# A flow backbone with three attention groups: transposes of each block of keys issued ahead of its predecessor's products, in groups B and C

## The chip, the cores and the metric

The kernel runs on one core of a Trainium2 chip. The metric is device time in microseconds (us) for one execution; less is better. Before the change the median of three runs is 1200.18 us (1199.35 to 1202.86).

## The reference

Two trunk layers work on 512 latent tokens (a grid of 8 rows by 64 columns) and 256 context tokens, each 1024 wide. A layer normalises and modulates both streams, projects them to queries, keys, values and gates, runs three groups of attention heads side by side, multiplies by a SiLU gate, projects back and adds. Context reads context alone; latents read their own keys and all context keys in one softmax. The second layer needs no context output.

```python
def layer(x, cx, ...):
    px, pc = split_cols(hx @ w_in), split_cols(hc @ w_in)
    ya, yca = global_gqa(...)          # A: 8 heads, 2 of keys; all 512 + 256 keys
    yb, ycb = neighbourhood_attn(...)  # B: 8 heads; 8 x 16 window with bias, + 256 keys
    yc_, ycc = window_gqa(...)         # C: 8 heads, 2 of keys; +-128 tokens, sink, + 256 keys
    ux = jnp.concatenate([ya, yb, yc_], -1) * jax.nn.silu(px[9])
    x = x + gate * (ux @ w_out)
```

All is in float32.

## The kernel before

**Precision.** A float32 operand that goes through TensorE is split in two of a faster type, a rounded part (names ending in h, or index x = 0) and the rest (l, or x = 1). So one float32 product is two or three matmuls.

**Stages.** `PLAN` (line 33) lists the stages of a layer. In each stage the attention of one pair of heads runs (B pairs 0 to 3, then A and C in turn: A0, C0, A1, C1, A2, C2, A3, C3) and beside it the projections that a later stage needs: beside B those of further B pairs and the first A pair, beside A those of a C pair, beside C those of an A pair. `weave` (line 1407) takes from the two generators in proportion to the microseconds that each of their steps yields. Behind the last stage the output projection starts (`head`, line 527).

**A unit.** A pair of heads is cut in units (`units`, line 1288): for each head one unit of 512 latent queries in B (`NearUnit`) and C (`BandUnit`), two units of 256 in A (`GlobalUnit`), and in the first layer one unit for the context queries (`CtxUnit`). A unit has two generators. `scores` makes the scores in PSUM (tile `Sbig`), their row minimum or maximum and the exponentials in SBUF (tile `P`, 128 queries each, five buffers). `values` turns them round and multiplies by the values. `attend` (line 1375) zips the values of one unit with the scores of the next.

**Values.** Keys come in six blocks of 128; blocks 4 and 5 are the context. For each block, the parts of `P` that have keys in it are transposed on TensorE into a PSUM bank (`turn`, line 1053; tile `T`, two banks, `psT`, line 96). `pt_copy` (line 1039) moves the bank to SBUF in two halves: ScalarE (ACT) copies the rounded half, `pth`, and VectorE (DVE) takes the difference, `ptl`, which needs the first. Three buffers hold each half. `pv` (line 1058) then multiplies the block's values by both halves into the accumulator `Obig`, one PSUM bank for all units. A block of group B has four query tiles (context) or two; one of C has four (context), two or three. `o_out` (line 1069) folds the two halves of the accumulator when the sixth block is done. The helper functions `mul` and `turn` record every product and every transpose, so in the profile all products stand at L1049 and all transposes of this kind at L1054; they are told apart by tiles.

The T banks are shared. The query transposes of an A pair's projection (`a_pair`, line 883, transposes at L899, copied out by ACT at L902 into tile `qt`) take one too, and so do `finish` (line 1315) and, once a layer, the keys of A and the values of C.

**Order.** The program is written with one issue order, but each engine's queue is laid out before the run by a planner that simulates a timeline (line 1666): the issue order is its priority, and where an instruction would not be ready in the simulation, a later one can go first. Some orders are fixed by hand with `after` (line 99): projections may not run further ahead of the attention than `lead` allows (lines 296 and 1407). On the chip every queue keeps the order that was laid out.

**Ahead.** The helper `ahead` (line 1098) takes steps of turns, sums and a time. It issues the turns of a step, yields, issues the sums of the step before, and yields. Only group A uses it before the change. In B and C a block's transposes and copies are issued, then a yield, then the same block's products, then a yield.

Of the kernel before, what the change touches and what calls it, by code (L numbers as in the profile page):

```python
# [771 lines left out]
def mixers(tc, nc, l, last, p1, ps, const, env):  # L772
# [19 lines left out]
    turns = {}  # L792

    def copy(out, src, kind):

        n = turns[kind] = turns.get(kind, -1) + 1
        if CFG[kind][n % len(CFG[kind])] == "A":
            nc.scalar.activation(out, src, AF.Copy)  # L798
        else:
            nc.vector.tensor_copy(out, src)  # L800
# [238 lines left out]
    def pt_copy(T, n):  # L1039

        hi = p1.tile([128, 512], F32R, name="pth", bufs=CFG["pt"])
        lo = p1.tile([128, 512], F32R, name="ptl", bufs=CFG["pt"])
        copy(hi[:, 0:n], T[:, 0:n], "cp")
        i = nc.vector.tensor_sub(lo[:, 0:n], T[:, 0:n], hi[:, 0:n].bitcast(F32))  # L1044
        pace["dve"] = i.ins.name
        return hi, lo

    def mul(*args, **kw):
        m = nc.tensor.matmul(*args, **kw)  # L1049
        pace["pe"] = m.ins.name  # L1050
        return m

    def turn(*args, **kw):
        m = nc.tensor.transpose(*args, **kw)  # L1054
        pace["pe"] = m.ins.name
        return m

    def pv(O, v, pt, o, c0, n, first, final):

        for x in range(2):  # L1060
            a = mul(O if c0 is None else O[:, c0:c0 + n], v, pt[x][:, o:o + n], start=first and x == 0,
                                 stop=final and x == 1, skip_group_check=True)

            if first and x == 0 and "last" in opv:
                after(a, opv["last"])
            if final and x == 1:
                opv["last"] = a.ins.name

    def o_out(O, OT, h, c0, n):
        tmp = p1.tile([64, 512], F32, name="otmp", bufs=1)  # L1070
        nc.scalar.activation(tmp[:, 0:n], O[64:128, 0:n], AF.Copy)
        nc.vector.tensor_add(OT[64 * h:64 * h + 64, c0:c0 + n], O[0:64, 0:n], tmp[:, 0:n])
# [25 lines left out]
    def ahead(steps):  # L1098


        late = None
        for turns, sums, t in steps:
            pt = turns()
            yield t
            if late:
                late[0](late[1])
                yield late[2]
            late = sums, pt, t
        late[0](late[1])
        yield late[2]  # L1110

    class CtxUnit(Unit):
# [18 lines left out]
        def values(self):  # L1131
            T = psT()
            for kb in range(2):
                for t in range(2):
                    turn(T[:, (2 * kb + t) * 128:(2 * kb + t + 1) * 128],
                                        self.P[:, t * 256 + kb * 128:t * 256 + (kb + 1) * 128], ident)
            pt = pt_copy(T, 512)
            yield 0.45
            O = half_O()
            for kb in range(2):  # L1140
                pv(O, self.v(4 + kb), pt, kb * 256, 0, 256, kb == 0, kb == 1)
            o_out(O, self.OT(), self.h, NT, NCX)
            yield 0.45
# [41 lines left out]
    class BandUnit(Unit):  # L1185
# [32 lines left out]

        def values(self):
            O = psO()  # L1220
            for n, kb in enumerate((4, 5, 0, 1, 2, 3)):
                qs = [i for i in range(4) if kb in self.pos[i]]
                T = psT()
                for j, i in enumerate(qs):
                    o = self.pos[i][kb]
                    turn(T[:, j * 128:(j + 1) * 128], self.P[i][:, o:o + 128], ident)
                k = len(qs) * 128
                pt = pt_copy(T, k)
                yield k / 1200
                pv(O, self.v(kb), pt, 0, qs[0] * 128, k, n == 0, n == 5)  # L1230
                yield k / 1200
            o_out(O, self.OT(), self.h, 0, NT)

    class NearUnit(Unit):
# [36 lines left out]

        def values(self):
            O = psO()
            for n, kb in enumerate((4, 5, 1, 2, 3, 0)):
                qs = [i for i in range(4) if kb in self.PLAN[i][4]]
                T = psT()
                for j, i in enumerate(qs):
                    o = self.PLAN[i][4][kb]
                    turn(T[:, j * 128:(j + 1) * 128], self.P[i][:, o:o + 128], ident)
                k = len(qs) * 128  # L1280
                pt = pt_copy(T, k)
                yield k / 1200
                out = O[:, qs[0] * 128:qs[0] * 128 + k] if kb else O.rearrange("p (t c) -> p t c", t=4)[:, 0:4:3]
                pv(out, self.v(kb), pt, 0, None, k, n == 0, n == 5)
                yield k / 1200
            o_out(O, self.OT(), self.h, 0, NT)

    def units(kind, i, Q, K, V, G, extra):
# [242 lines left out]
    for pair, items, n_ada in PLAN:  # L1531
# [3 lines left out]
        if pair is not None:  # L1535
            kind, i = pair
# [13 lines left out]
        t = sum(time[k] for k, i in items)  # L1550
# [120 lines left out]
```

## Time and profile before

| | us |
|---|---|
| median of three runs | 1200.18 |
| lowest, highest run | 1199.35, 1202.86 |
| span of the profiled execution | 1197.7 |
| TensorE busy | 1150.5 |
| TensorE weight loads | 1034.8 |
| VectorE busy | 769.4 |
| ScalarE busy | 696.9 |
| GpSimd busy | 408.1 |

The span is what the profile shows of its one execution, from the first to the last instruction; the time of a run has in addition what lies around it, and the lowest of the three is 1.65 us above the span, the median 2.5 us. In the rows of the profile, PE is TensorE (PEld its weight loads, which overlap with its matmuls), DVE is VectorE, ACT is ScalarE, POOL is GpSimd and SP issues DMAs. A row of the timeline has the start, the duration, the engine, the line, the operation, the tile written and the tiles read, the shape, how many instructions were merged, and in brackets the idle time of the engine before it and what ended that. Matmuls are pipelined: their ends are modelled, and one that follows another starts before the other's end. So a short stall of TensorE doesn't always appear as idle time.

### The profile page before, as it was taken

What the parts mean: (1) busy time and instruction counts of PE and PEld (TensorE: products, weight loads), DVE (VectorE), ACT (ScalarE), POOL (GpSimd) and SP (SyncE); (2) the same over time, 40 slices, a digit from 0 to 9 for tenths busy, and PEclk for the clock granted to TensorE, in tenths of its full rate; (3) what the DMA queues carried; (4) which work ended last, traced back from release to release, by engine and by line L of the source; (5) the groups of instructions that cost most, each with busy time, mean ns of one, the idle gap of its engine ahead of it and who ended that gap; (6) DMA issues with size and microseconds to landing.
All of it is one profiled execution on the core that took longest, in us unless ns stands there. A gap on an engine that the chain in (4) does not pass through costs nothing.

```text
span 1197.7 us, 21749 instructions
## 1 busy us (share of the span) xinstructions
PE 1150.5 (96%) x8016; PEld 1034.8 (86%) x8016; DVE 769.4 (64%) x1548; ACT 696.9 (58%) x1581; POOL 408.1 (34%) x496
## 2 busy tenths in 40 slices
PE   5999999999999999999999999999999999998997
PEld 3898999998898988988778999989988888887876
DVE  5767566764656665568578895567754556567563
ACT  5446555656666676588423544555666667677552
POOL 1341110234446354385000030202274563656001
PEclk9999999999999999999999999999999999999999
DMA  9552222313312112123086662323222111232152
GB/s 321 213 142 89 78 78 67 123 66 104 111 70 92 67 44 92 34 63 119 27 293 198 205 210 74 98 84 109 91 73 67 53 46 53 63 88 72 36 161 77
DMA packets 60826, 124.22 MB, mean 104 GB/s; under 512 B 7216, under 2 KB 13488, under 8 KB 60720
## 3 DMA queue, kind: packets, MB, share of 16 engines
q1 hardware_dynamic: 54768, 111.96, 29.6%
q10 hardware_dynamic: 5952, 10.88, 2.7%
q8 instruction: 63, 1.03, 0.3%
q14 instruction: 43, 0.35, 0.1%
HBM read 109.05 MB, written 11.14 MB: 100 GB/s over the span
## 4 chain that ended last, share of the span: by engine, by line
PE 81%; DVE 5%; ACT 5%; DMA 3%; issue 3%; POOL 1%; SPq 0%; ACTq 0%; DVEq 0%; POOLq 0%
PE pj L318 18%; PE pj L341 17%; PE Sbig L1049 9%; PE Obig L1049 9%; PE T L1054 9%; PE pj L519 5%; PE T L519 3%; PE Sbig L519 3%; PE T L341 2%; PE Sbig L430 2%; DVE ptl L1044 1%; DMA x<-xT_dram 1%; PE Sbig L341 1%; ACT pth L798 1%; PE pj L430 1%
## 5 line engine op out<-in xcount | busy, mean ns | idle before, releaser
L1044 DVE TENSOR_TENSOR ptl<-T,pth 128x512 fp32r<-128x512 f32 (+2 forms) x312 | 181.1, 591 | 128.6 <-ACT pth L798 126.7
L798 ACT ACTIVATE pth<-T 128x512 fp32r<-128x512 f32 (+2 forms) x312 | 158.9, 520 | 134.8 <-PE T L1054 128.1
L341 PE MATMUL pj<-wh,hL 128*128 128x256 f32 x896 | 180.6, 287 | 0.0
L318 PE MATMUL pj<-hL,wh 128*128 128x512 f32 x544 | 175.0, 401 | 0.9 <-ACT wh L247 0.5
L1054 PE MATMUL T<-ident,P 128*128 128x128 f32 x1024 | 165.7, 273 | 4.0 <-ACT qt L902 1.7
L247 ACT ACTIVATE wh<-ws 128x512 fp32r<-128x512 f32 x192 | 119.5, 629 | 78.6 <-PE pj L318 16.3
L1049 PE MATMUL Sbig<-kt,qt 128*128 128x256 f32 (+1 forms) x864 | 156.2, 308 | 4.6 <-ACT P L1160 2.5
L250 POOL TENSOR_TENSOR wl<-ws,wh 128x512 fp32r<-128x512 f32 x76 | 98.5, 1300 | 146.4 <-ACT wh L247 146.4
L341 PEld LDWEIGHTS pj<-wh,hL 128*128 128x128 f32 x896 | 144.2, 190 | 1.0 <-issue 0.2
L1049 PE MATMUL Obig<-pth,vt 128*128 128x256 f32 (+2 forms) x432 | 134.6, 321 | 4.6 <-ACT pth L798 2.0
L1054 PEld LDWEIGHTS T<-ident,P 128*128 128x128 f32 x1024 | 123.0, 140 | 17.6 <-DVE ptl L1044 2.2
L1049 PE MATMUL Obig<-ptl,vt 128*128 128x256 f32 (+2 forms) x432 | 131.4, 318 | 5.0 <-DVE ptl L1044 4.3
L1049 PEld LDWEIGHTS Sbig<-kt,qt 128*128 128x128 f32 x864 | 123.3, 189 | 13.4 <-DVE negm L1208 4.1
L341 PE MATMUL pj<-wl,hL 128*128 128x256 f32 x448 | 128.0, 286 | 0.0
L318 PEld LDWEIGHTS pj<-hL,wh 128*128 128x128 f32 x544 | 96.2, 189 | 16.7 <-ACT wh L247 0.9
L250 DVE TENSOR_TENSOR wl<-ws,wh 128x512 fp32r<-128x512 f32 x116 | 82.7, 720 | 40.4 <-ACT wh L247 31.6
L318 PE MATMUL pj<-hL,wl 128*128 128x512 f32 x272 | 107.1, 394 | 0.5 <-DVE wl L250 0.5
L1049 PEld LDWEIGHTS Obig<-pth,vt 128*128 128x128 f32 x432 | 81.6, 189 | 15.9 <-ACT pth L798 7.1
L1049 PEld LDWEIGHTS Obig<-ptl,vt 128*128 128x128 f32 x432 | 81.5, 189 | 14.7 <-DVE ptl L1044 11.3
L1445 POOL TENSOR_TENSOR bm<-wr,bm 128x192 f32<-128x192 f32 (+1 forms) x48 | 41.3, 888 | 139.6 <-DMA bm<-mskB_dram 132.4
L341 PEld LDWEIGHTS pj<-wl,hL 128*128 128x128 f32 x448 | 85.4, 191 | 0.3
L1158 DVE TENSOR_REDUCE negm<-Sbig 128x1 f32<-128x768 f32 x64 | 61.0, 953 | 29.7 <-PE Sbig L1049 15.7
(336 smaller groups left out, 2495.6 us busy)
## 6 DMA issues: line engine op xcount, KB each, us to landing
ws<-wf_dram SPq DMA_DIRECT2D x72, 256.0 KB, 3.1
ws<-wt_dram SPq DMA_DIRECT2D x72, 256.0 KB, 3.0
ada<-adaw_dram SPq DMA_DIRECT2D x32, 512.0 KB, 5.5
ws<-wo_dram SPq DMA_DIRECT2D x57, 256.0 KB, 2.8
bm<-mskB_dram SPq DMA_DIRECT2D x16, 576.0 KB, 3.7
dw<-adat_dram SPq DMA_DIRECT2D x8, 512.0 KB, 8.2
dots<-adat_dram SPq DMA_DIRECT2D x16, 256.0 KB, 4.5
u<-u ACTq DMA_DIRECT2D x9, 384.0 KB, 2.9
```

Of the source, the lines that this page charges most:

```text
L247: nc.scalar.activation(hi, src, AF.Copy)
L250: eng.tensor_sub(lo, src, hi.bitcast(F32))
L318: paced(nc.tensor.matmul(p[:, 0:n], a[:, r, :], cols(b[kt], c0, n), start=(i == 0), stop=(i == 23)), i)
L341: paced(nc.tensor.matmul(p[:, t * 256:(t + 1) * 256], tok(a[kt], t2 + t), b[:, r, :], start=(i == 0), stop=(i == 23)), i)
L430: mm = nc.tensor.matmul(out, a, b, start=begin, stop=(kt == KT - 1 and i == 2), skip_group_check=True)
L519: mm = nc.tensor.matmul(p[:, 0:n], a[:, r, :], ucols(ua[b][ft], c0, n), start=(ft == FT_ORDER[0] and i == 0), stop=(ft == FT_ORDER[-1] and ...
L798: nc.scalar.activation(out, src, AF.Copy)
L1044: i = nc.vector.tensor_sub(lo[:, 0:n], T[:, 0:n], hi[:, 0:n].bitcast(F32))
L1049: m = nc.tensor.matmul(*args, **kw)
L1054: m = nc.tensor.transpose(*args, **kw)
L1158: nc.vector.tensor_reduce(nm, S, axis=AX.X, op=OP.max, negate=True)
L1445: nc.gpsimd.tensor_add(b, src, b)
```

## The change

In the latent units of B (`NearUnit`) and C (`BandUnit`), `values` now hands its six blocks to `ahead`. The transposes and copies of block n + 1 are issued before the products of block n. The blocks, their order, their tiles, the flags of the accumulation and the yielded times stay. Group A and the context units are not touched.

```diff
@@ BandUnit (group C) @@
         def values(self):
             O = psO()
-            for n, kb in enumerate((4, 5, 0, 1, 2, 3)):
-                qs = [i for i in range(4) if kb in self.pos[i]]
+            order = (4, 5, 0, 1, 2, 3)
+            tiles = {kb: [i for i in range(4) if kb in self.pos[i]] for kb in order}
+
+            def turns(kb):
                 T = psT()
-                for j, i in enumerate(qs):
+                for j, i in enumerate(tiles[kb]):
                     o = self.pos[i][kb]
                     turn(T[:, j * 128:(j + 1) * 128], self.P[i][:, o:o + 128], ident)
-                k = len(qs) * 128
-                pt = pt_copy(T, k)
-                yield k / 1200
-                pv(O, self.v(kb), pt, 0, qs[0] * 128, k, n == 0, n == 5)
-                yield k / 1200
+                return pt_copy(T, len(tiles[kb]) * 128)
+
+            def sums(kb, pt):
+                pv(O, self.v(kb), pt, 0, tiles[kb][0] * 128, len(tiles[kb]) * 128, kb == order[0], kb == order[-1])
+
+            yield from ahead([(lambda kb=kb: turns(kb), lambda pt, kb=kb: sums(kb, pt), len(tiles[kb]) * 128 / 1200)
+                              for kb in order])
             o_out(O, self.OT(), self.h, 0, NT)
```

`NearUnit` (group B) is changed in the same way, with its own order of blocks (4, 5, 1, 2, 3, 0); there the last block's products go to the first and the fourth query tile. The helper, which stood already:

```python
def ahead(steps):
    late = None
    for turns, sums, t in steps:
        pt = turns()
        yield t
        if late:
            late[0](late[1])
            yield late[2]
        late = sums, pt, t
    late[0](late[1])
    yield late[2]
```

More of the change, by code (lines that the diff above doesn't have):

```diff
@@ L1273, in values, with turns, sums @@
             O = psO()
-            for n, kb in enumerate((4, 5, 1, 2, 3, 0)):
-                qs = [i for i in range(4) if kb in self.PLAN[i][4]]
+            order = (4, 5, 1, 2, 3, 0)
+            tiles = {kb: [i for i in range(4) if kb in self.PLAN[i][4]] for kb in order}
+            def turns(kb):
                 T = psT()
-                for j, i in enumerate(qs):
+                for j, i in enumerate(tiles[kb]):
                     o = self.PLAN[i][4][kb]
                     turn(T[:, j * 128:(j + 1) * 128], self.P[i][:, o:o + 128], ident)
[L1280 to L1285, printed above, removed]
+                return pt_copy(T, len(tiles[kb]) * 128)
+            def sums(kb, pt):
+                q0, k = tiles[kb][0] * 128, len(tiles[kb]) * 128
+                out = O[:, q0:q0 + k] if kb else O.rearrange("p (t c) -> p t c", t=4)[:, 0:4:3]
+                pv(out, self.v(kb), pt, 0, None, k, kb == order[0], kb == order[-1])
+            yield from ahead([(lambda kb=kb: turns(kb), lambda pt, kb=kb: sums(kb, pt), len(tiles[kb]) * 128 / 1200)
+                              for kb in order])
             o_out(O, self.OT(), self.h, 0, NT)
```

## The prediction

> **What bounds the kernel now.** I read the page first, then the waits of TensorE, then its busy time stage by stage, then the timeline of a few blocks.
>
> ```profile
> span 1197.7 us, 21749 instructions
> ...
> PE 1150.5 (96%) x8016; PEld 1034.8 (86%) x8016; DVE 769.4 (64%) x1548; ACT 696.9 (58%) x1581; POOL 408.1 (34%) x496
> ...
> PEclk9999999999999999999999999999999999999999
> ...
> PE 81%; DVE 5%; ACT 5%; DMA 3%; issue 3%; POOL 1%; SPq 0%; ACTq 0%; DVEq 0%; POOLq 0%
> ```
>
> TensorE (PE) is the bound: 96% busy at the full granted clock, and 81% of the chain that ended last. So an edit that neither adds nor removes TensorE work can win only what TensorE stands idle, 1197.7 - 1150.5 = 47.2 us in all. Some of that is start and end. The waits of TensorE for the whole program (waiter, whom for, us in total, times, longest) say which part this change can touch:
>
> ```profile
> PE Obig L1049 <- DVE ptl L1044: 4.3, 11, 0.8
> ...
> PE Obig L1049 <- ACT pth L798: 2.0, 6, 0.5
> ...
> PE T L1054 <- DVE ptl L1044: 1.8, 3, 0.9
> PE T L1054 <- ACT qt L902: 1.7, 2, 1.2
> ```
>
> The first two are products that wait for the two halves of their transposed block (pth by ACT, ptl by DVE). The last two are transposes that wait for a T bank. The list leaves out short gaps, so I take the idle time itself, per stage. Groups B and C run separately from A in time, so windows cut along the products of each head pair separate them. The five answers below are, in this order: C of layer 0 (341 to 374, 420 to 450, 497 to 528, 569 to 600), C of layer 1, A of layer 0 (290 to 338, 379 to 415, 456 to 493, 533 to 567), A of layer 1 (908 to 945, 975 to 1004, 1032 to 1062, 1093 to 1118), and B of both layers. In a row stand the window, its length and TensorE's busy time.
>
> ```profile
> sum 125.00, PE 120.07; mean PE 30.02
> ```
>
> ```profile
> 947.00:971.00 24.00, 21.83 (x139) 1.00 0.22 68
> 1005.00:1029.00 24.00, 22.14 (x136) 1.00 0.23 67
> 1063.00:1090.00 27.00, 25.89 (x145) 1.00 0.46 133
> 1120.00:1143.00 23.00, 22.18 (x121) 1.00 0.18 58
> sum 98.00, PE 92.04; mean PE 23.01
> ```
>
> ```profile
> sum 155.00, PE 152.02; mean PE 38.00
> ```
>
> ```profile
> sum 121.00, PE 117.79; mean PE 29.45
> ```
>
> ```profile
> 101.00:286.00 185.00, 184.97 (x1394) 1.00 0.27 85
> 756.00:905.00 149.00, 147.37 (x1053) 1.00 0.30 89
> ```
>
> Idle time is length less busy: C 4.93 us in layer 0 (3.9%) and 5.96 us in layer 1 (6.1%); A 2.98 us (1.9%) and 3.21 us (2.7%); B 0.03 us and 1.63 us (1.1%). So C has 10.89 us, B 1.66 us, and 12.55 us is all that this change can win directly. Group A already issues its blocks in the new order, through the same helper and with the same two T banks, which makes it the nearest row for what the order is worth.
>
> **What one stall looks like.** Layer 1, second head of the first C pair:
>
> ```profile
> 962.24 0.60 PE L1054 MATMUL T<-ident,P 128*128 128x128 f32 x4
> 962.52 0.69 DVE L1044 TENSOR_TENSOR ptl<-T,pth 128x512 fp32r<-128x512 f32 x1 [0.25 <-ACT pth L798]
> 962.59 0.48 PE L1049 MATMUL Obig<-pth,vt 128*128 128x512 f32 x1
> 962.87 0.60 ACT L798 ACTIVATE pth<-T 128x512 fp32r<-128x512 f32 x1 [0.39 <-PE T L1054]
> 963.26 0.19 PEld L1049 LDWEIGHTS Obig<-ptl,vt 128*128 128x128 f32 x1 [0.51 <-DVE ptl L1044]
> 963.26 0.50 PE L1049 MATMUL Obig<-ptl,vt 128*128 128x512 f32 x1 [0.19 <-DVE ptl L1044]
> 963.50 0.69 DVE L1044 TENSOR_TENSOR ptl<-T,pth 128x512 fp32r<-128x512 f32 x1 [0.29 <-ACT pth L798]
> ```
>
> The transposes of 962.24 end at 962.84. Their ACT half ends at 963.47 and their DVE half at 964.19, that is 1.35 us later. TensorE has to find 1.35 us of other work between a block's transposes and its second product. Note also that these transposes are those of the second block and stand ahead of the first block's products (962.59) already; the product at 963.26 waited all the same.
>
> **The change, part by part.**
>
> Instructions: none is added, removed or resized. Every B or C unit keeps 16 or 18 transposes, six pairs of copies and twelve products. Cost 0, and no DMA or SP or POOL queue is passed. The yields that share out the projections beside a unit add up to the same sum.
>
> The order of issue: a block's products now come behind the next block's transposes and one more share of projection. In the rows above, what follows four transposes starts 0.35 us after them (962.24 to 962.59). That is a quarter of the 1.35 us, and the yield of 512/1200 = 0.43 us in the code makes room for about as much projection. So products that now wait a few tenths of a microsecond should mostly find their copies done. What they wait for next is the copy itself when ACT or DVE is late with other work.
>
> But issue order is only a priority here: a planner lays out each queue before the run. The first pair of blocks of group B, and two pairs that lie the other way, in TensorE's timeline:
>
> ```profile
> 97.13 0.87 PE L1054 MATMUL T<-ident,P 128*128 128x128 f32 x6
> ...
> 101.24 0.40 PE L1049 MATMUL Obig<-pth,vt 128*128 128x512 f32 x1
> ...
> 944.55 0.60 PE L1054 MATMUL T<-ident,P 128*128 128x128 f32 x4
> ...
> 947.90 0.40 PE L1049 MATMUL Obig<-pth,vt 128*128 128x512 f32 x1
> 948.14 0.46 PE L899 MATMUL T<-identr,qd 128*128 128x128 f32 x4
> 948.43 0.46 PE L1049 MATMUL Obig<-ptl,vt 128*128 128x512 f32 x1
> 948.74 0.60 PE L1054 MATMUL T<-ident,P 128*128 128x128 f32 x4
> 950.49 0.44 PE L1054 MATMUL T<-ident,P 128*128 128x128 f32 x2 [1.15 <-ACT qt L902]
> 950.97 0.51 PE L1049 MATMUL Obig<-pth,vt 128*128 128x512 f32 x1
> ...
> 1140.86 0.44 PE L1054 MATMUL T<-ident,P 128*128 128x128 f32 x2
> 1141.05 0.42 PE L1049 MATMUL Obig<-ptl,vt 128*128 128x384 f32 x1
> 1141.31 0.34 PE L1049 MATMUL Obig<-pth,vt 128*128 128x384 f32 x1
> ```
>
> At 97.13 four transposes of the first block and two of the second stand ahead of the first product at 101.24: already the new order. At 947.90 the product comes before the second block's transposes (948.74): the old order. The last pair, 1140.86 ahead of 1141.31, is in the new order again. Counted so from the first of these pairs to the last, 114 of the 160 pairs of B and C (30 and 26 of 40 in B, 31 and 27 of 40 in C) already have transposes ahead, against 58 of 64 in A. So the change turns round about 46 pairs, and pushes the products of the others a little further back.
>
> Term 1, group C. Bounds: nothing (the planner does it already) and a gain of all 10.89 us; a loss can only come through the banks, which is term 3. I take A's idle share, the nearest row with this order: layer 0, 1.9% of 125 is 2.4, a gain of 2.5 us; layer 1, 2.7% of 98 is 2.6, a gain of 3.4 us. Together 5.9 us.
>
> Term 2, group B. Layer 0 has 0.03 us of idle time and gives nothing: its projections cover everything. Layer 1 with 1.1% already lies under A's share; bounds 0 and 1.63, I take 0.4.
>
> Term 3, the T banks. There are two. With the order of A, both are filled sooner in a C unit. C has a neighbour that A has not: the projection of the next A pair, whose query transposes (the row at 948.14) need a T bank too and hold it until ACT has copied them out. The wait of 1.15 us at 950.49 is just that. All such transposes of the program:
>
> ```profile
> L899 PE MATMUL T<-identr,qd x80: 222/246/278, 258.4 to 1075.5; 128*128 128x128 f32 x80
> ```
>
> Four share a bank, so 20 groups; by the plan of stages 5 of them lie beside B and 15 beside C. Two cost a wait now, 1.7 us together. Bounds for the change: 1.7 us gained (both gone) and 15 x 1.15 - 1.7 = 15.6 us lost (every one meets it). I take one more wait, rounded to 1.0 us lost, since two in 15 is the present rate and the order of the units moves by a fraction of a block.
>
> [...]
>
> Sum: -5.9 - 0.4 + 1.0 = -5.3 us on the profiled span, 1197.7 to 1192.4. The median of the runs is 1200.18, 2.5 us above that span, and I carry this difference along: 1194.9, said as 1195.
>
> **The rivals.**
>
> *The order was there already.* For it: 114 of 160 pairs, and the stall at 963.26, which came in spite of it. Then only the 22 of 80 pairs of C that lie the other way are improved: 22/80 of 10.89 is 3.0 us, less the 1.0 of term 3, which gives 1198. If the two banks were all that holds C, not even that would come: 1200, by the waits for a bank (3.5 us against 6.3 us for copies) a third of this rival's chance. Against it: A, with the same copies and a higher share of pairs ahead, idles half as much. A difference under 0.3% (3.6 us) is about what a measurement of this kernel can't tell from none, so this rival means 1196.6 to 1203.8.
>
> *Slower: T banks taken by C while the next A pair's queries want them.* Place: C of layers 0 and 1, beside the projections of A pairs 1 to 3. Price: 1.15 us at a time, with TensorE at a stand, since nothing behind the blocked transpose starts. It decides once it eats the gain and 3.6 us more, 6.3 + 3.6 = 9.9 us, which is 9 further groups of the 13 that run free now. With 11 of them the sum is 12.7 - 6.3 = +6.4 us, some 1206. For it: both waits of this kind stand in C of layer 1, where units follow most closely. Against it: layer 0 has nine of the fifteen and no such wait.
>
> [...]
>
> **How the numbers follow.** Forecast of a gain over 3.6 us: 0.50; order already there: 0.31; slower: 0.19. The forecast is likeliest, as the 10.89 us is really idle time on the bounding engine and A shows half of it away; it isn't higher because a gain of 3.6 needs more than half of term 1, and each new layout of the queues shifts other waits. Its own range runs from all direct idle time gone, 1200.2 - 12.5 = 1187.7, to the edge at 1196.6. For 8 in 10 I take 1188 to 1204: all of the second case, and of the slower one just the edge.
>
> **What would show it.** Right: idle time of C's windows falls from 10.9 to about 5 us, that of B in layer 0 stays at nil, the products' waits for pth and ptl fall from 6.3 to about 3 us, and the count of pairs ahead rises to A's nine in ten. Busy time and instruction counts stay. Term 3 is wrong if transposes wait for qt in more than three or four places. The prediction is wrong if C's idle time stays above 9 us, or falls and comes back elsewhere: in A, in scores that wait for Sbig, or at the end behind the last C unit.

## The result, and the profile after

After the change the median is 1209.42 us (five runs, 1206.04 to 1209.86), against 1200.18 before. The ratio is 1.0067 with a 95% interval of 1.0052 to 1.0082: slower by 9.2 us between the medians, 8.0 us by the ratio, where the prediction had 5 us faster. The profiled span went from 1197.7 to 1207.2 us, 9.5 us more.

The page of the kernel after: span, busy times, and the start of the chain that ended last.

```profile
span 1207.2 us, 21759 instructions
...
PE 1152.4 (95%) x8016; PEld 1036.1 (86%) x8016; DVE 771.1 (64%) x1548; ACT 695.5 (58%) x1581; POOL 406.2 (34%) x496
```

The same 8016 matmuls, as predicted. TensorE's busy time, which was to stay, grew by 1.9 us and its idle time from 47.2 to 54.8 us, so of the 9.5 us 7.6 are waiting. The waits of TensorE after (waiter, whom for, us in total, times, longest):

```profile
PE Obig L1049 <- DVE ptl L1044: 5.1, 10, 1.5
PE T L1054 <- DVE ptl L1044: 4.0, 6, 1.3
PE Obig L1049 <- ACT pth L798: 3.7, 8, 1.1
...
PE T L341 <- DVE wl L250: 1.6, 1, 1.6
PE T L341 <- DVE xn L587: 1.6, 1, 1.6
```

The products' waits for the two copied halves, which were to fall from 6.3 to about 3 us, rose to 8.8. Transposes that wait for a T bank which an earlier block's copies hold (second row) went from 1.8 to 4.0 us, and those that wait for `qt` (1.7 us before) are gone. The last two rows are new and lie in the output projection.

Where the time arose shows in windows cut at the first or last product of a stage: B of layer 0, A and C of layer 0, the output projection up to layer 1's first product, the attention of layer 1. Each row has the window, its length and TensorE's busy time; then the granted clock. First before, then after.

```profile
101.00:290.00 189.00, 188.97 (x1424) 1.00 0.26 84
290.00:600.00 310.00, 302.09 (x2183) 1.00 0.23 72
600.00:756.00 156.00, 152.14 (x985) 0.99 0.60 193
756.00:1143.00 387.00, 375.12 (x2540) 1.00 0.24 71
```

```profile
100.00:293.00 193.00, 192.68 (x1444) 1.00 0.27 85
293.00:605.00 312.00, 301.19 (x2162) 0.99 0.22 70
605.00:765.00 160.00, 152.13 (x989) 1.00 0.58 188
765.00:1152.00 387.00, 374.33 (x2537) 1.00 0.24 71
```

Read length less busy, not length: the new layout also does 20 matmuls more in the first window and 21 less in the second. Idle time goes from 0.03 to 0.32, from 7.91 to 10.81, from 3.86 to 7.87 and from 11.88 to 12.67 us, that is +0.3, +2.9, +4.0 and +0.8; the start and the end of the program gave a little back. The largest part lies in the output projection, ahead of the first product of layer 1, where no product of B or C lies.

The same cut as in the prediction, pair by pair, for the kernel after: C of layer 0, C of layer 1, A of layer 0, A of layer 1, and B of both layers.

```profile
sum 122.00, PE 115.38; mean PE 28.84
```

```profile
sum 93.00, PE 87.23; mean PE 21.81
```

```profile
sum 153.00, PE 149.27; mean PE 37.32
```

```profile
sum 123.00, PE 119.06; mean PE 29.76
```

```profile
100.00:284.00 184.00, 183.90 (x1388) 1.00 0.27 86
765.00:913.00 148.00, 146.26 (x1048) 1.00 0.30 89
```

C idles 6.62 and 5.77 us: 12.4 in all, where 10.9 was to become 5. A, which the change doesn't touch, went from 2.98 to 3.73 and from 3.21 to 3.94.

**Did the order change?** Yes. Counted as in the prediction, the blocks of B and C with the next block's transposes ahead of their products rose from 30 and 26 of 40 (B) to 38 and 36, and from 31 and 27 of 40 (C) to 36 and 33. The change does what it says; it isn't worth what was expected.

Idle time misses short stalls, as matmuls overlap: in the prediction's rows the transposes of 948.14 end at 948.60, and the next matmul starts at 948.43. From here on, a stall is the time from the end of the previous matmul to a matmul's own end, less the median of that for its shape. Summed so, the products of B and C lost 16.7 us before and 13.6 after: the change bought 3.1 us at its own products. But before the change the 46 blocks that it could turn round held only 1.5 us of stall; 13.1 us lay at blocks with transposes ahead already, the rest at the last block of a unit.

### The profile page after: what moved, and what is told of

The parts are those of the page before. It is cut to its first block, busy times and chain, and to the rows that moved or that the text cites. A ratio compares the mean times of both kernels' runs of the same rounds, so it can differ in the third digit from the quotient of the medians.

```text
span 1207.2 us, 21759 instructions
## 1 busy us (share of the span) xinstructions
PE 1152.4 (95%) x8016; PEld 1036.1 (86%) x8016; DVE 771.1 (64%) x1548; ACT 695.5 (58%) x1581; POOL 406.2 (34%) x496
## 5 line engine op out<-in xcount | busy, mean ns | idle before, releaser
L1054 PE MATMUL T<-ident,P 128*128 128x128 f32 x1024 | 166.6, 274 | 5.0 <-DVE ptl L1044 3.5
L1054 PEld LDWEIGHTS T<-ident,P 128*128 128x128 f32 x1024 | 123.6, 141 | 18.6 <-DVE ptl L1044 3.6
```

## The experiments

All of them are the kernel after with a switch that says in which group and layer the new order is used (`inturn` is the old order: turns, yield, sums, yield). Ratios are to the kernel before in the same session, with 95% intervals.

```diff
+AHEAD = (("B", 1), ("C", 1))
...
-            yield from ahead([...
+            yield from (ahead if ("C", l) in AHEAD else inturn)([...
```

The theories were these. Theory 1: the change's own gain is small, and the loss comes because the planner lays the queues out anew, in stages that the change doesn't touch too. Theory 2: the new order itself costs, by its use of the two T banks.

### Which part costs

New order in layer 1 alone, in layer 0 alone, in C alone, in B alone:

> New order in both groups, in the second layer alone; TensorE's queue is that of the kernel before up to the first B unit of layer 1. Theory 1 (knock-on: the new order wins a little in its own units, and the loss comes from other stages that the planner lays out differently, and from the halved clock behind their stalls): the losses of layer 0 (5.7 us) and of the output projection behind it (3.2 us) are gone; what stays is what layer 1 showed, 2 to 3 us won in C and 2.7 us lost in the last A stage, so 1196 to 1201 us. Theory 2 (the new order itself costs, by its use of the two T banks): about half of the 9 us lost, 1204 to 1206 us.

> New order in both groups, in the first layer alone. Theory 1: layer 0 and the projection behind it are laid out as in the changed kernel, so most of the loss is here, 1206 to 1211 us, while the products' waits in B and C of layer 0 are no longer than before. Theory 2: the other half, 1204 to 1206 us, with more waits for T banks in layer 0.

> New order in group C alone, both layers. Theory 1: the stalls before products of C fall by 1 to 3 us; the total depends on a new layout and can be anywhere from 1196 to 1210 us; it need not add up with the run of group B. Theory 2: C shares its T banks with the query transposes of A pairs, B hardly does, so C brings most of the loss: 1206 to 1210 us, and C and B add up to the whole.

> New order in group B alone, both layers. TensorE idled 0.03 us and 1.63 us in B, so there is next to nothing to win or to lose in place. Theory 1: a time more than 3.6 us from 1200 us, on either side, with B's own windows unchanged, would be layout alone; 1196 to 1210 us. Theory 2: 1199 to 1202 us.

| new order in | median | ratio |
|---|---|---|
| layer 1 (B, C) | 1200.32 | 0.9998 (0.9986 to 1.0010) |
| layer 0 (B, C) | 1212.85 | 1.0096 (1.0077 to 1.0115) |
| C, both layers | 1205.22 | 1.0041 (1.0026 to 1.0056) |
| B, both layers | 1202.47 | 1.0005 (0.9994 to 1.0016) |

Layer 0 costs, layer 1 doesn't. Layer 0 alone came out above what either theory expected. The parts don't add up: the median of layer 0 alone is above that of the whole change (their intervals touch), and C's 0.41% with B's 0.05% are well short of layer 0's 0.96%. Part of that lies in the last A stage of layer 1, whose order this kernel doesn't change: 30.4 us against 26.7 before (last section). Two further runs took C of one layer alone:

> The new order in group C of layer 0 alone; everything else in the old order. Both theories put the loss here, and C of layer 1 (in e3_group_c with it) ran its stages behind layer 1's first B stage in 439.7 us against 441.3 before, a gain of 1.6. If the two add, this kernel is slower than e3_group_c by that much: 1200.2 + 4.9 + 1.6, about 1206.5, with the layer-0 attention ending near 606 us of the span as in e3_group_c (599.6 before). Theory 1 (knock-on: the new order is laid out differently around it) allows anything from 1201 to 1207; theory 2 (the new order itself costs, by its use of the two T banks) wants at least 1204.

> The new order in group C of layer 1 alone, the part whose stages got shorter. If its 1.6 us stand alone: 1198.6, ratio about 0.9987, the stages of layer 1 from its first B stage to the end 439.7 us against 441.3 before. Both theories allow it; if it comes out at 1200 or above, a gain in its own stages is given back even here. It is the candidate for a version that is faster than both kernels.

C of layer 0 alone: 1207.24 us, 1.0053 (1.0036 to 1.0070). C of layer 1 alone: 1200.53 us, 0.9994 (0.9984 to 1.0004). In its trace the stages C0, A1, C1 and A2 of layer 1, each from its first product to that of the next, take 24.5 + 32.2 + 24.7 + 32.9 = 114.3 us against 27.2 + 30.3 + 27.4 + 30.9 = 115.8 before, with the same lengths to 0.1 us as in the kernel with C in both layers. But stage A3, in which a stretch at half clock falls (last section), takes 28.6 us against 26.7 and gives it back. It is no version that is shown to be faster.

### The same work, laid out otherwise

The weight with which layer 0's projections are woven in is 2.7. Another weight changes no work and lets the planner lay out the same program differently.

```diff
-    TC = 0.0 if last else 2.7
+    TC = 0.0 if last else 2.6
```

First 2.6 and 2.8, in the old order and with the whole change:

> Old order everywhere; only the weight that shares out the projections beside the attention of layer 0 is 2.6 in place of 2.7. The same instructions, another layout of the queues. Theory 1 (the layout of other stages decides the microseconds): anywhere from 1196 to 1208 us, and away from the twin with 2.8 by some microseconds. Theory 2 (the new order itself costs 9 us): within 2 us of 1200 us.

> Old order, weight 2.8. Theory 1: 1196 to 1208 us, other than the twin with 2.6. Theory 2: within 2 us of 1200 us.

> New order in both groups and layers, weight 2.6. Theory 1: 1198 to 1212 us; the families of old and new order overlap. Theory 2: 1207 to 1211 us, like the changed kernel.

> New order, weight 2.8. Theory 1: 1198 to 1212 us. Theory 2: 1207 to 1211 us.

They came out at 1200.26 and 1202.89 in the old order, 1206.88 and 1206.31 in the new one. That looked like theory 2: two families, at least 3.4 us apart. But 2.6 had left most of the queue as it was: a line-by-line comparison of the tiles of TensorE's matmuls, in the order of the traces, has 262 lines of difference from before, where the change itself makes 2258. So these were hardly four independent layouts. 2.4 and 3.0 (936 and 1694 lines) went further, now with the new order in C of layer 0 alone, where the cost had been found:

> The old order throughout, the weight of layer 0's weave 2.4 instead of 2.7 (another layout of the queue, the same work). Theory 2 (the new order itself costs): 1199 to 1203, as the other old layouts (1200.3 and 1202.9). Theory 1 (layouts differ by some 5 us, whatever the order): anything from 1198 to 1208.

> Weight 2.4, the new order in C of layer 0 alone. Theory 2: 4 to 6 us above p24_old, with 1.5 us or more of transposes that wait for a T bank in C of layer 0, and A and C of layer 0 together 25 us or more of stalls (21 to 22 in the old layouts). Theory 1: as likely below p24_old as above it.

> The old order throughout, weight 3.0, the layout farthest from before. Theory 2: 1199 to 1204. Theory 1: anything from 1198 to 1208.

> Weight 3.0, the new order in C of layer 0 alone. Theory 2: 4 to 6 us above p30_old. Theory 1: as likely below p30_old as above it; a pair in which the new order is 2 us or more below the old one ends theory 2 in its form 'whatever the layout'.

| weight | old order | new order | new less old |
|---|---|---|---|
| 2.4 | 1205.86, 1.0041 (1.0026 to 1.0055) | 1206.78, 1.0041 (1.0028 to 1.0054), C of layer 0 | +0.9 |
| 2.6 | 1200.26, 0.9995 (0.9982 to 1.0007) | 1206.88, 1.0045 (1.0030 to 1.0060), all | +6.6 |
| 2.7 | 1200.18, before | 1209.42, 1.0067 (1.0052 to 1.0082), all | +9.2 |
| 2.8 | 1202.89, 1.0019 (1.0008 to 1.0030) | 1206.31, 1.0042 (1.0025 to 1.0059), all | +3.4 |
| 3.0 | 1209.25, 1.0063 (1.0045 to 1.0081) | 1206.87, 1.0043 (1.0028 to 1.0059), C of layer 0 | -2.4 |

Theory 2 in its form "whatever the layout" wanted the new order 4 to 6 us above the old at 2.4 and at 3.0; the differences of +0.9 and -2.4 end it. At 3.0 the two intervals overlap, so that the new order is faster there isn't shown. The old order alone spreads over 9 us with the weight, and at 3.0 it is above what either theory expected. Whether a weight far from 2.7 also shares out the projections worse by itself was not separated from its being another layout. TensorE in the A and C stages of layer 0, for 2.4 old and new, then 3.0 old and new:

```profile
291.00:608.00 317.00, 305.74 (x2192) 0.99 0.23 71
```

```profile
291.00:607.00 316.00, 305.82 (x2194) 1.00 0.22 71
```

```profile
295.00:610.00 315.00, 302.79 (x2164) 1.00 0.22 70
```

```profile
293.00:607.00 314.00, 302.33 (x2168) 0.99 0.22 70
```

Idle: 11.26, 10.18, 12.21 and 11.67 us, all like the 10.81 of the kernel after, two of them in the old order. The old order at 2.6 (7.50), 2.7 (7.91) and 2.8 (9.14) has less. In the output projection, too, the old order at 3.0 idles 6.4 us, against 3.9 before and 7.9 after. Nor do waits for a bank need the new order: transposes wait for `ptl` for 4.7 us in the old order at 2.4 and 5.2 us at 2.8, where the kernel after has 4.0; of these, transposes of `P` in C of layer 0 have 2.9, 3.1 and 2.3 us.

### Banks that come free earlier

In this pair DVE's half of C's copies is left out in layer 0, so a T bank is free when ACT's copy ends. The old order is in the first, the new order in C of layer 0 in the second.

```diff
     def pt_copy(T, n, whole=False):
...
+        if whole:
+            return hi, hi
         i = nc.vector.tensor_sub(lo[:, 0:n], T[:, 0:n], hi[:, 0:n].bitcast(F32))
```

> The old order throughout, with the low half of C's probabilities left out in layer 0: both products of a key tile take the rounded half that ACT copies, and DVE's subtraction of the low half is not issued, so a T bank comes free at the end of ACT's copy. It is the base for h_new_half_c0. Both theories: C's product waits for ptl in layer 0 (3.2 us) fall away, and DVE has some 80 instructions of 0.5 to 1.2 us less beside C: 1193 to 1200.

> The same without the low half of C's probabilities in layer 0, but with the new order in C of layer 0. Theory 2 (banks): with the banks free after ACT's copy, the transposes ahead of the products no longer wait for T, so the new order costs nothing any more: 0 to 2 us below h_old_half, and no wait of C's transposes for a copy in layer 0 above 1 us in all. Theory 1 (the queue around C is laid out anew, and what that gives is a matter of the layout): the difference of the two is not tied to the banks; 3 us or more to either side with no bank waits would speak for it, as would a loss of 4 to 6 us as in e3_group_c.

Old order: 1206.10 us, 1.0043 (1.0028 to 1.0058). New order: 1204.47 us, 1.0030 (1.0020 to 1.0040). Two things follow. With early banks the new order loses nothing against the old one, as theory 2 had it; a bank wait is a real cost (1.06 us in the dearest case, see "Why the prediction was wrong"). But the old order lost 5 us although work was taken away from it, and in the places of the kernel after: the stalls in A of layer 0 sum to about 10 us before, 14 after and 14 here, and grew by the same waits: for `OT` 1.8, 2.7 and 2.3 us, for `ptl` 1.4, 2.3 and 2.1, for `hL` from GpSimd 0, 1.2 and 1.0. So that loss needs no new order. The windows of A and C in layer 0, old and then new:

```profile
291.00:606.00 315.00, 303.76 (x2180) 0.99 0.23 71
```

```profile
291.00:602.00 311.00, 302.11 (x2183) 1.00 0.23 72
```

They idle 11.24 and 8.89 us. The expectation of 1193 to 1200 for the old order was missed. DVE's copies in C of layer 0, which it put at 0.5 to 1.2 us each, take 0.41 to 0.69 us in the kernel before.

### The order without the planner's timeline

One switch of the planner turns off the simulated timeline, so that the queues follow priorities and dependencies alone.

```diff
-CFG = dict(..., tl=1, ...)
+CFG = dict(..., tl=0, ...)
```

> The old order with the scheduler's timeline off (tl=0): the order of the queue comes from priorities and dependencies alone. Both theories: slower than before by far, 1250 us or more, since the timeline is what interleaves the units to due times; more stalls of B's and C's products behind their own copies than before (the four classes together 17 us before).

> The new order in B and C of both layers with the timeline off. If the mechanism is sound and only the scheduler had taken it already: faster than q_old_notime by up to 160 blocks of 0.1 to 0.3 us, 15 to 50 us. If the order doesn't pay at all: within 5 us of it or slower.

Old order: 1379.93 us. New order: 1368.76 us, 11.2 us less; their ratios to before, 1.1491 (1.1457 to 1.1525) and 1.1397 (1.1374 to 1.1420), don't overlap. The waits of TensorE's products for the copied halves, old and then new (line numbers are one higher in these files):

```profile
PE Obig L1050 <- ACT pth L799: 12.8, 9, 3.6
...
PE Obig L1050 <- DVE ptl L1045: 6.8, 9, 4.2
```

```profile
PE Obig L1050 <- ACT pth L799: 8.0, 8, 2.4
PE Obig L1050 <- DVE ptl L1045: 6.8, 4, 2.9
```

Here 67 of 160 blocks of B and C had the next transposes ahead in the old order, and 151 in the new. Those that lay the other way held 12.0 us of stall in the old order, and all product stalls of B and C fell from 27.7 to 15.6 us, by 12.1, close to the 11.2 measured. So the mechanism works in this pair. Other waits moved with it (the query transposes' wait for `qd` from GpSimd rose from 49.0 to 54.7 us), so it may be chance that the two figures meet so closely. It came out under the 15 to 50 us expected, and in the real kernel the timeline had taken most of it already.

## Why the prediction was wrong

**TensorE is the bound; nothing is added:** right, and it is why the losses show as TensorE's waiting or as its half clock. Its busy time did not stay, though: the one more stretch at half clock (0.50 for 3.4 us) comes to some 1.7 of the 1.9 us, by estimate.

**Count of blocks, nine in ten after:** right, 143 of 160.

**Term 1, gain of 5.9 us in C: this is the step that failed.** It took C's idle share as something the order sets, and A's share as what the order is worth. C's idle time stayed, 12.4 us after 10.9. A stage's idle time is not the stall of the blocks that a change turns round; that stall could have been summed from the trace before, and was 1.5 us in B and C together, 0.6 of it in C. The pair without the timeline shows the other side: where such blocks hold 12.0 us, the order wins 11.2. The prediction's own example, the product at 963.26 that waited although transposes stood ahead of it, was the evidence. It was used for the rival, and term 1 was sized as if it were not there.

**Term 2, gain of 0.4 us in B:** missed. B of layer 1 idles 1.74 us after 1.63, B of layer 0 0.10 after 0.03. B alone measures as no change.

**Term 3, T banks, a loss of 1.0 us:** the size was near, the place wrong. Waits for a bank went from 1.8 + 1.7 us to 4.0, half a microsecond more, but none is for the queries' `qt` any more. They are for `ptl`, the copies of earlier blocks, and 2.3 us of them are in C of layer 0. The old order at 2.4 and 2.8 waits there as much, so even this isn't the new order's own. The dearest shape of it, in C of layer 0 after the change:

```profile
439.91 0.69 DVE L1044 TENSOR_TENSOR ptl<-T,pth 128x512 fp32r<-128x512 f32 x1
...
441.84 0.68 DVE L1044 TENSOR_TENSOR ptl<-T,pth 128x512 fp32r<-128x512 f32 x1
...
442.67 0.52 PE L1054 MATMUL T<-ident,P 128*128 128x128 f32 x3 [1.06 <-DVE ptl L1044]
...
442.94 0.48 PE L1049 MATMUL Obig<-pth,vt 128*128 128x512 f32 x1
```

The first block's halves are done at 440.60, so its product could run. But the planner has put the transposes of the third and the fourth block ahead of it, the fourth's wait for a bank until the second block's `ptl` is out (442.52), and the product stands behind them until 442.94. The issue order of the change asks for one block ahead; this is three.

**A term that was missing.** The sum had no entry for what a new layout does elsewhere; term 1 said that a loss can only come through the banks, and new layouts stood only as a reason against a higher chance. This was the largest term: +4.0 us of idle time in the output projection, +2.9 in A and C of layer 0, and one window more at half clock. In layer 1 the stages from the first B to C2 are 2.2 us shorter than before, but A3, which the change doesn't touch, is 2.7 us longer and takes that back; another order of A3's instructions is not the reason (last section). In the output projection the two new waits of 1.6 us (for `wl` and `xn`) also appear with the new order in layer 0 alone (1.5 and 1.2 us) and with the change at weight 2.6 (1.4 and 1.5), smaller with the change at weight 2.8 and in the new order with early banks. They are in no old-order kernel, and in none with the whole computation that has the new order in C alone. In the kernel after DVE stands idle ahead of the normalisation, behind a dot product of its own queue:

```profile
701.25 0.75 DVE L153 CUSTOM_DVE_ANT_0 junk<-dots,mod 128x512 bf16<-128x512 f32 x1 [4.87 <-issue]
```

That this dot, put earlier in the queue, is what makes the normalisation late is argued from the row and was not tested.

**The rivals.** "The order was there already" was right about the mechanism and wrong about the time, since it took the rest of the program as unmoved. "Slower: T banks" had the sign and a near time (1206), but not the cause: its `qt` waits are gone. The range ended at 1204 because it gave the second case, which changes nothing, no price for a new layout.

That the two banks are all that holds C, which had a third of the first rival's chance, is borne out in part: with early banks the new order costs nothing against the old (1204.47 us after 1206.10). The layouts at 3.0 speak against it: there the new order shows no cost with the banks as they are (1206.87 us after 1209.25).

**What stays open.** Over the five weights the new order is on average 3.6 us slower (1203.7 against 1207.2), with differences from -2.4 to +9.2, in a mixture of the whole change and its part in C of layer 0; five such pairs can't tell this from nothing. In the profiled executions of the pairs at 2.6, 2.7 and 2.8 the new order lost 2.6, 2.7 and 3.6 us in A3 of layer 1 alone (last section); those at 2.4 and 3.0 lost nothing there. That before is among the best of the five old layouts is shown; that the new order has no good one is not, as weights beyond these weren't tried.

## What to carry to other kernels

To price a change of order, sum the stalls at exactly those instructions that it turns round, and not the idle time of the stage they lie in; where a planner lays out the queues, most of them may have been turned round before. In this kernel, whose bounding engine is 96% busy, another layout of the same work moved the time by up to 9 us, more than the edit could win by its own stalls: before reading a result of half a per cent as the edit's own, lay out old and new several times with some knob that changes no work, and compare the two spreads. A change that helps a plain queue (here 0.8%) may be worth nothing behind a planner.

## What the runs showed of the hardware

**Half a clock after a bad window.** In the last A stage of layer 1 the kernel after loses more than its stalls. TensorE's clock in two successive stretches of 3.4 us:

```profile
1102.70:1106.10 3.40, 1.49 (x9) 1.00 0.01 2
1106.10:1109.50 3.40, 3.20 (x13) 0.50 0.00 0
```

In the second stretch four transposes take 1.05 us where they take 0.60 in the first, so some 1.7 us of work are lost (3.4 us at 0.50 of the clock, an estimate). In the clock records of before and after, each stretch at 0.50 ahead of the last 6 us of the program lasts 3.413 us (one and two of them). Ahead of the output stage such windows come at 563.4 and 1106.1 us in the kernel after, 542.7 us apart, which is 159 times 3.413; without the timeline they are many, and their distances of 17.1 and 61.4 us are 5 and 18 times that. So a grid of 3.413 us fits them, an estimate from these distances. The window ahead of that at 1106.1 was not idle: TensorE was busy for 1.49 of its 3.40 us, and the longest idle time in it is the 1.53 us below, which reaches a little beyond its end. In the fourteen traces with the planner's timeline that have such a window, cut on this grid from 70 us to the output stage, the window ahead of a half-clock one held 1.95 us of stalls or more, and every window at full clock with over 2.16 us was followed by one (a stall lies right behind the previous matmul's end). So in these traces several short stalls close together cost up to 1.7 us more, by where they fall on the grid. The kernel before has one of these windows (at 625.2 us), that after two.

**A race of 50 ns between DVE and GpSimd.** What made that window bad, in the kernel after:

```profile
1102.95 2.95 POOL L990 TENSOR_TENSOR qt<-tR,qt 64x512 fp32r<-64x512 f32 x2
1103.00 1.78 DVE L492 TENSOR_TENSOR ut<-u,ut 128x512 fp32r<-128x512 f32 x1
...
1103.55 0.60 PE L1054 MATMUL T<-ident,P 128*128 128x128 f32 x4
...
1105.57 1.27 DVE L1044 TENSOR_TENSOR ptl<-T,pth 128x512 fp32r<-128x512 f32 x2
...
1106.30 0.58 PE L1049 MATMUL Obig<-ptl,vt 128*128 128x256 f32 x1 [1.53 <-DVE ptl L1044]
...
1107.10 1.05 PE L1054 MATMUL T<-ident,P 128*128 128x128 f32 x4
```

The same code in the kernel with the new order in layer 1 alone (line numbers one higher). From the first product of A2 to the last product of the layer, its instructions on TensorE, DVE, ACT and GpSimd stand in the same order, by tile and shape, as in the kernel after:

```profile
1094.52 0.68 DVE L493 TENSOR_TENSOR ut<-u,ut 128x512 fp32r<-128x512 f32 x1
1094.59 3.10 POOL L991 TENSOR_TENSOR qt<-tR,qt 64x512 fp32r<-64x512 f32 x2
...
1096.80 0.39 PE L1050 MATMUL Obig<-ptl,vt 128*128 128x256 f32 x1 [0.72 <-DVE ptl L1045]
```

Where DVE started 0.07 us ahead of GpSimd it took 0.68 us; where GpSimd was 0.05 us ahead it took 1.78, the next `ptl` came later, and TensorE's wait was 1.53 instead of 0.72 us. A3, from its first product to that of C3, takes 29.4 us in the one and 26.7 in the other. Why DVE's instruction is the longer one there is not shown. In twelve of the eighteen traces with the planner's timeline DVE starts 0.07 us ahead, and A3 takes 26.5 to 26.8 us. In five (the kernel after, the change at weights 2.6 and 2.8, the new order in layer 0 alone and in C of layer 0 alone) GpSimd is 0.05 to 0.78 us ahead, that DVE instruction takes 1.04 to 1.78 us, and A3 takes 29.3 to 30.4 us, half-clock windows included. In the last (C of layer 1 alone) they start together, and A3 takes 28.6. The two that change only layer 0 have A3's instructions in the order of the kernel before, so the race is lost in the old order too. All five have the new order in C of layer 0, but four others with it don't lose the race; what tips it is open, and no run moved one instruction alone.

**The split's faster type.** In the kernel before, a 128x128 transpose of float32 (`T<-ident,P`, L1054) takes 273 ns in the mean of 1024, and one of the rounded type (`T<-identr,qd`, L899) 240 ns in the mean of 80 (`identr` and `qd` are of the rounded type, though the rows print f32).
